# The first expert's seven chunks stand twice, in an If for up to 64 tokens and in an Else for more

## The chip, the cores and the metric

The kernel runs on one core of a Trainium2 chip. The metric is the device time of one execution, in microseconds (us). TensorE is written PE (its weight loads PEld, its sequencer PEq), VectorE DVE, ScalarE ACT, GpSimd POOL, and SP is the engine that issues the weight transfers. A profile is one execution under the hardware profiler.

## The reference, cut to what matters

The model is a two-layer decoder trunk over 256 tokens of width 1024. The change touches its last sublayer alone, a mixture of eight experts of which each token takes two:

```python
D_MODEL = 1024; SEQ = 256; N_EXPERTS = 8; TOP_K = 2; D_FF_EXPERT = 3584

def _swiglu(x, w1, w3, w2):
    return (jax.nn.silu(x @ w1) * (x @ w3)) @ w2

def _moe(x, w_router, w1, w3, w2):
    logits = (x @ w_router).astype(jnp.float32)
    top_v, top_i = lax.top_k(logits, TOP_K)
    gates = jax.nn.softmax(top_v, axis=-1)
    gate_full = jnp.sum(jax.nn.one_hot(top_i, N_EXPERTS, dtype=jnp.float32) * gates[..., None], axis=-2)
    out = jnp.zeros_like(x)
    for e in range(N_EXPERTS):
        y = _swiglu(x, w1[e], w3[e], w2[e])
        out = out + gate_full[..., e, None].astype(x.dtype) * y
    return out
...
        x = _layer_norm(DEEPNORM_ALPHA * x + f, ln_g[i, 1], ln_b[i, 1])
```

All weights are float32. The expert weights alone are 336 pieces of 1 MiB (128 x 2048 floats). With the reference's inputs the router sends 45, 78, 50, 86, 62, 60, 65 and 66 tokens to experts 0 to 7.

## The kernel before, in words

Everything ahead of the experts (state-space layer, dense feed-forward, attention) is left as it is. The stage in question is `experts` and the router code just ahead of it.

**Slots.** The tokens of an expert are gathered into a fixed number of slots, so that the matmuls have a fixed shape. Expert 0 is always taken first, with 96 slots. Experts 1 to 7 are sorted by their token counts while the kernel runs and put in places 1 to 7, whose slots are 64, 96, 64, 96, 96, 96, 64 (`CAPS`). If a place overflows, further passes at the end (an If on `cint[8]`) do the rest; that doesn't happen here.

**Chunks.** Each expert is cut in seven chunks (`NJ`) of 512 hidden columns, 56 in all, numbered `n`. A chunk takes six pieces: two of w1 and two of w3 (`up(n, 0, b)`, `up(n, 1, b)`), two of w2 (`down(n, b)`). With `b = 0` the first 64 slots are computed. An expert with 96 slots also has `b = 1` for the last 32 (`rest` for the up part). ACT takes the silu, DVE the product (`gated`), PE turns the result with transposes (`flip`, tile `ht`), and ACT copies it to `h`. The chunks overlap: `up` of chunk n stands ahead of `down` of chunk n-1.

**Pieces.** `Stream` holds a ring of 17 buffers `raw` (the tile `xx` is one of them, once). `take` hands out the next piece in order, `back` returns a buffer after its last matmul, and `load` issues the next transfer into it (line 74, on SP's queue, in the order of the program). The pieces of expert 0 have fixed addresses. Those of the other places depend on the sorting: `order` computes their starts into `cint`, and SP reads seven registers from there (line 1228) before it issues anything more.

**Around it.** After the router, `gather(0)` brings expert 0's tokens in with 32 matmuls (tile `gx`, line 1336). Small steps are kept in the list `side`, and `aside` runs one or two in each chunk: `gates`, `counts` (a matmul `cn` against ones and the first half of the sorting), `order`, `back` (for the scatter), the eight steps of `gather(1)` for places 1 to 4 and of `gather(2)` for places 5 to 7, and four `scatter` steps per finished expert. In chunk 5, POOL and ACT make the residual `x1` (lines 1472, 1473).

Of the kernel before, what the change touches and what calls it, by code (L numbers as in the profile page):

```python
# [45 lines left out]
class Stream:  # L46
# [31 lines left out]
    def add(self, raw=(), pairs=()):  # L78
        self.free.extend(raw)
        self.pairs.extend(pairs)  # L80
        self.load()

# [54 lines left out]
def trunk(ctx: ExitStack, tc: tile.TileContext, a, out, dbg=None):  # L137
# [45 lines left out]
    for n in range(E * NJ + 1):  # L183
        for m, qs in ((n, range(4)), (n - 1, (4, 5))):
            if 0 <= m < E * NJ:
                moe_seq += [(piece(m // NJ, 6 * (m % NJ) + q), 2048, False) for q in qs]
# [791 lines left out]
    with ExitStack() as e:  # L978
# [200 lines left out]
        cint = mo.tile([1, 9], I32, name="cint")  # L1179
# [22 lines left out]
        def counts(pp):  # L1202

            o = pp.tile([128, 8], F32, tag="tt", name="cn")
            for t in range(2):
                T.matmul(o, lhsT=ones, rhs=mask[:, t, :], start=(t == 0), stop=(t == 1))
            V.tensor_copy(out=by_e[:, 6, :], in_=o)
# [102 lines left out]
    def experts(ws, pas, pyy):  # L1310
        if pas:
            V.tensor_tensor(out=by_i[:, 2:4, :], in0=by_i[:, 2:4, :], in1=cst[:, None, 24:32].to_broadcast([128, 2, 8]), op=S_)
        with ExitStack() as e:
            pa = e.enter_context(pool(f"ps_a{pas}", bufs=1, space=PSUM))
            pto = None if pas else e.enter_context(pool("ps_to", bufs=1, space=PSUM))
            ptt = e.enter_context(pool(f"ps_tt{pas}", bufs=2, space=PSUM))
# [41 lines left out]

            def up(n, i, b):
# [8 lines left out]
                for hf in range(2):  # L1368
                    w = got[n, i][hf].rearrange("p (k c) -> p k c", c=512)
                    for k in range(4):  # L1370
                        kk = 4 * hf + k
                        tiles(ob[n, i], oc, x_[:, kk, x0 + lo:x0 + lo + m], w[:, k, :], m, 4 * m, not b and kk == 0, kk == 7)
                    if b or CAPS[n // NJ] == 64:
                        ws.back(got[n, i][hf])
                        ws.load()

            def flip(n):
                h_, q = hTs[n % 2], 3 if CAPS[n // NJ] > 64 else 2
# [5 lines left out]
            def down(n, b):  # L1384
                ee, j = divmod(n, NJ)
                h_ = hTs[n % 2]
                if b == 0:
                    got[n, 2] = [ws.take() for _ in range(2)]
                    if j == 0:
                        yp[ee] = [pyy.tile([128, 512 // (i + 1)], F32, tag=f"y{i}", name=f"y{i}") for i in range(2)]  # L1390
                for hf in range(2):
# [5 lines left out]
                    if b or CAPS[ee] == 64:  # L1397
                        ws.back(got[n, 2][hf])
                        ws.load()
# [17 lines left out]
            if pas:  # L1417
# [5 lines left out]
            def gated(n, i):  # L1423

                c, sl = 384 if CAPS[n // NJ] > 64 else 256, sls[n % 2]
# [5 lines left out]
            for n in range(NS + 1):  # L1431
                ee, j = divmod(n, NJ)
                big, bigp = (0 <= m < NS and CAPS[m // NJ] > 64 for m in (n, n - 1))

                def rest():
                    for i in range(2):
                        up(n, i, 1)
                        gated(n, i)

                if n < NS:  # L1440
                    up(n, 0, 0)
                    if not big:
                        gated(n, 0)
                if 0 < n < NS:
                    flip(n - 1)
                for _ in range(3 if n == 0 else 2):
                    aside()
                if n < NS:
                    up(n, 1, 0)
                    if not big:  # L1450
                        gated(n, 1)
                if n == NS - 1:
                    if big:
                        rest()
                    if not spare:
                        nc.sync.dma_start(out=ws.free[0], in_=gain_bias(3))
                        spare.extend(ws.free.pop(0).rearrange("p (a b) -> p a b", a=2) for _ in range(2))
                if n > 0:
                    down(n - 1, 0)
                    if n == NS - 1:  # L1460
                        flip(n)
                    if bigp:
                        down(n - 1, 1)
                    if (n - 1) % NJ == NJ - 1:
                        pe = (n - 1) // NJ
                        if pe < E - 1 or pas:
                            side.extend(out_steps(pe, yp.pop(pe)))
                if big and n < NS - 1:
                    rest()
                if n == 5 and not pas:  # L1470
                    for t in range(2):
# [5 lines left out]
                if j == 1 and ee + 1 < E:  # L1477
                    side.append(lambda q=ee + 1: back(q))
            while side:
                aside()  # L1480
            return yp.get(E - 1)
# [174 lines left out]
```

## Time and profile before

| | us |
|---|---|
| median of 3 runs (1542.08 to 1545.64) | 1544.24 |
| the profiled execution's own time | 1542.1 |
| its span, first to last instruction | 1540.2 |
| expert 0's first matmul starts | 674.5 |
| expert 0's first 17 pieces are issued by | 663.3 |
| the 18th piece is issued | 687.1 |
| PE busy over the span | 1465.0 |

The profile page has the span cut in 40 slices, with what the DMA engines moved in each. The trace behind it can be asked for the busy time of any stretch, for the instructions in order of time with what ended the idle time before each, and for one source line.

### The profile page before, as it was taken

What the parts mean: (1) busy time and instruction counts of PE and PEld (TensorE: products, weight loads), DVE (VectorE), ACT (ScalarE), POOL (GpSimd) and SP (SyncE); (2) the same over time, 40 slices, a digit from 0 to 9 for tenths busy, and PEclk for the clock granted to TensorE, in tenths of its full rate; (3) what the DMA queues carried; (4) which work ended last, traced back from release to release, by engine and by line L of the source; (5) the groups of instructions that cost most, each with busy time, mean ns of one, the idle gap of its engine ahead of it and who ended that gap; (6) DMA issues with size and microseconds to landing.
All of it is one profiled execution on the core that took longest, in us unless ns stands there. A gap on an engine that the chain in (4) does not pass through costs nothing. (4 is left out here: it accounts for less than half of the span.)

```text
span 1540.2 us, 34541 instructions
## 1 busy us (share of the span) xinstructions
PE 1465.0 (95%) x15235; PEld 1069.0 (69%) x15235; DVE 546.0 (35%) x1019; ACT 385.5 (25%) x633; POOL 117.5 (8%) x156
## 2 busy tenths in 40 slices
PE   7769899997999999999999999999899999999995
PEld 6657799996999999866665566654566666566552
DVE  9998844447566555541011010010100100100103
ACT  6525434333555545420010000010000100100100
POOL 0010573005000000000100000000000000000001
PEclk9989999999999999999999999999999999999998
DMA  6018389653535544458899999999999999989995
GB/s 254 7 35 298 143 279 255 205 183 139 181 135 181 178 151 173 162 237 365 329 375 426 426 426 424 425 426 426 426 424 426 424 390 400 390 350 389 397 426 220
DMA packets 68417, 458.41 MB, mean 298 GB/s; under 512 B 9041, under 2 KB 9716, under 8 KB 15780
## 3 DMA queue, kind: packets, MB, share of 16 engines
q1 hardware_dynamic: 62752, 443.63, 72.2%
q0 software_dynamic: 4272, 9.92, 2.3%
q10 hardware_dynamic: 1236, 2.58, 0.5%
q8 instruction: 122, 2.00, 0.5%
q14 instruction: 35, 0.29, 0.1%
HBM read 454.97 MB, written 3.48 MB: 298 GB/s over the span
## 5 line engine op out<-in xcount | busy, mean ns | idle before, releaser
L1356 PE MATMUL a<-raw,xe 128*32 128x128 f32 (+1 forms) x8016 | 537.7, 322 | 5.3 <-DMA raw<-in_moe 3.5
L1356 PEld LDWEIGHTS a<-raw,xe 128*32 128x32 f32 (+1 forms) x8016 | 371.9, 122 | 157.4 <-issue 28.6
L1356 PE MATMUL y<-raw,h 128*32 128x256 f32 (+1 forms) x2016 | 267.8, 476 | 2.9 <-DMA raw<-in_moe 2.4
L1429 DVE TENSOR_TENSOR sl<-sl,a 128x384 f32<-128x384 f32 (+1 forms) x56 | 28.3, 505 | 580.1 <-PE a L1356 579.8
L96 DVE TENSOR_TENSOR sp<-raw,sp 128x2048 fp32r<-128x2048 f32 (+1 forms) x83 | 181.7, 2195 | 98.1 <-ACT sp L95 98.1
L1356 PEld LDWEIGHTS y<-raw,h 128*32 128x32 f32 (+1 forms) x2016 | 96.8, 122 | 154.8 <-issue 123.6
L95 ACT CAST sp<-raw 128x2048 fp32r<-128x2048 f32 (+1 forms) x85 | 154.3, 1823 | 69.8 <-PE ab L911 32.8
L1085 PE MATMUL qkp<-xT,sp 128*128 128x256 f32 x1152 | 153.1, 287 | 0.0
L1427 ACT ACTIVATE sl<-a 128x384 f32<-128x384 f32 (+1 forms) x56 | 25.3, 451 | 507.4 <-PE a L1356 507.3
L1085 PEld LDWEIGHTS qkp<-xT,sp 128*128 128x128 f32 x1152 | 141.9, 191 | 1.9
L911 PE MATMUL ab<-xT,sp 128*128 128x256 f32 x960 | 117.2, 283 | 0.0
L911 PEld LDWEIGHTS ab<-xT,sp 128*128 128x128 f32 x960 | 116.6, 192 | 0.8
L955 PE MATMUL pv<-sp,xT 128*128 128x384 f32 x384 | 73.6, 345 | 3.7 <-ACT xT L782 2.0
L1382 ACT COPY h<-ht 128x384 f32<-128x384 f32 (+1 forms) x56 | 24.6, 439 | 200.8 <-PE ht L1381 200.1
L955 PEld LDWEIGHTS pv<-sp,xT 128*128 128x128 f32 x384 | 67.5, 193 | 6.6 <-DVE xT L783 3.5
L742 POOL TENSOR_TENSOR lr__1387<-lr__1387,mhalf 128x1 f32<-128x1 f32 x8 | 4.6, 569 | 849.4 <-DVE lr__1387 L741 849.4
L899 PE MATMUL facc<-sp,hh 128*128 128x512 f32 x176 | 54.4, 390 | 0.0
L675 PE MATMUL glu<-sp,xT 128*128 128x512 f32 x144 | 36.0, 408 | 4.4 <-DVE sp L96 4.4
L1406 DVE SCALAR_TENSOR_TENSOR xx<-so,by_i,xx 128x512 f32<-128x512 f32 x28 | 19.7, 746 | 55.0 <-PE so L1405 55.0
L457 PE MATMUL pu<-x0T,raw 128*128 128x256 f32 x128 | 29.7, 394 | 8.3 <-DMA raw<-in_w_in 8.3
L899 PEld LDWEIGHTS facc<-sp,hh 128*128 128x128 f32 x176 | 32.4, 188 | 6.3
L675 PEld LDWEIGHTS glu<-sp,xT 128*128 128x128 f32 x144 | 28.0, 196 | 11.9 <-DVE sp L96 5.3
(269 smaller groups left out, 1174.1 us busy)
## 6 DMA issues: line engine op xcount, KB each, us to landing
raw<-in_moe SPq DMA_DIRECT2D x334, 1024.0 KB, 19.0
raw<-in_ffn SPq DMA_DIRECT2D x33, 1024.0 KB, 6.8
raw<-in_qk SPq DMA_DIRECT2D x24, 1024.0 KB, 4.8
raw<-in_wv SPq DMA_DIRECT2D x16, 768.0 KB, 4.1
raw<-in_w_glu SPq DMA_DIRECT2D x8, 1024.0 KB, 5.2
raw<-in_w_o SPq DMA_DIRECT2D x4, 1024.0 KB, 4.8
raw<-in_w_in SPq DMA_DIRECT2D x3, 1024.0 KB, 10.4
skew<-vecs POOLq DMA_DIRECT2D x64, 36.0 KB, 4.5
```

The source lines that it names most:

```text
L95: self.nc.scalar.copy(out=h_, in_=t_)
L96: (eng or self.nc.vector).tensor_tensor(out=l_, in0=t_, in1=h_, op=ALU.subtract)
L457: T.matmul(pu[:, mm].rearrange("p a b -> p (a b)"), lhsT=w[:, k, mm * 128:mm * 128 + 128], rhs=x0T[:, k, :], start=(k == 0 and mm == mms[0 ...
L675: T.matmul(o[t], lhsT=s_, rhs=m_, start=(kk == 0 and i == 0), stop=(kk == 7 and i == 2))
L899: T.matmul(acc[t][n], lhsT=s_, rhs=m_, start=(j == 0 and f == 0 and ip == 0), stop=(j == NFP - 1 and f == 1 and ip == 2))
L911: T.matmul(o[:, f, :], lhsT=s_, rhs=m_, start=(k == 0 and ip == 0), stop=(k == 7 and ip == 2))
L955: T.matmul(ov[t], lhsT=s_, rhs=m_, start=(kk == 0 and ip == 0), stop=(kk == 7 and ip == 2))
L1085: T.matmul(o[:, qk, :], lhsT=s_, rhs=m_, start=(k == 0 and ip == 0), stop=(k == 7 and ip == 2))
L1356: T.matmul(o[n * g:n * g + n, oc:oc + c], lhsT=lhsT, rhs=rhs[:, c * g:c * g + c], start=start, stop=stop, tile_position=(0, n * g), skip_g ...
L1382: A.copy(out=h_[:, 0:q], in_=p_[:, 0:q])
L1427: A.activation(out=sl[:, 0:c], in_=ob[n, 0][:, 0:c], func=ACTF.Silu)
L1429: V.tensor_tensor(out=sl[:, 0:c], in0=sl[:, 0:c], in1=ob[n, 1][:, 0:c], op=M_)
```

## The change

The seven chunks of expert 0 are written twice. The router's counts move ahead of the last transposes of the router stage, so that the count of expert 0 stands in `cint[9]` early. `gates`, the sorting (`places`, `order`) and the one-hots of places 1 to 4 are then written right behind `gather(0)`, ahead of the chunks. Every engine reads `cint[9]` into a register and branches. In the If (count below 65), the chunks are computed with 64 slots, the second result tile is set to zero, and the buffers are returned in the same order as in the Else, which computes 96 slots as before. Behind both, the pipeline starts anew: `x1`, then all of `gather(1)` in one block, then the scatter of expert 0 among the chunks of place 1. The last two w2 pieces of expert 0 are loaded ahead of the first four of place 1.

```diff
-        for m, qs in ((n, range(4)), (n - 1, (4, 5))):
+        for m, qs in ((n, range(4)), (n - 1, (4, 5)))[::-1 if n == NJ else 1]:
...
+        cn = sml[:, 288:296]
+        for t in range(2):
+            T.matmul(cn, lhsT=ones, rhs=mask[:, t, :], start=(t == 0), stop=(t == 1), skip_group_check=True)
         rows(1, 1, ptn, "tr")
...
         V.tensor_copy(out=rank, in_=rk)
+        V.tensor_copy(out=by_e[:, 6, :], in_=cn)
+        V.tensor_copy(out=cint[:, 9:10], in_=cn[0:1, 0:1])
         one_hots(0, by_e)
...
+            def chunks(n0, n1, few=False):
+
+                for n in range(n0, n1 + 1):
+                    ee, j = divmod(n, NJ)
+                    cap, capp = (CAPS[m // NJ] if 0 <= m < NS and not few else 64 for m in (n, n - 1))
+                    big, bigp = cap > 64, capp > 64
+
+                    def rest():
+                        for i in range(2):
+                            if big:
+                                up(n, i, 1)
+                                gated(n, i, 384)
+                            else:
+                                for hf in range(2):
+                                    give(n, i, hf)
...
-            side.extend([lambda: back(0)] if pas else [gates, lambda: counts(ptt), order, lambda: back(0)])
...
-                if n == 5 and not pas:
-                    for t in range(2):
-                        Q.tensor_tensor(out=x1[t], in0=xh[0][:, t, :], in1=xh[1][:, t, :], op=A_)
-                        A.mul(out=x1[t], in_=x1[t], mul=ALPHA)
-                if j == 1 and ee in (0, 2):
-                    g_ = gather(1 + ee // 2)
-                    side.extend([lambda q=1 + ee // 2, f=g_[0]: (one_hots(q), f()), *g_[1:]])
...
+                gates()
+                places()
+                order()
+                one_hots(1)
+
+                n0 = nc.values_load(cint[0:1, 9:10], min_val=0, max_val=256)
+                pools.close()
+                state = ws.state()
+                with tc.If(n0 < 65) as cmp:
+                    renew()
+                    V.memset(yp[0][1], 0.0)
+                    chunks(0, NJ, True)
+                    pools.close()
+                end = ws.state()
+                ws.set(state)
+                with cmp.Else():
+                    renew()
+                    chunks(0, NJ)
+                    pools.close()
+                assert ws.same(end)
+                renew()
+                for t in range(2):
+                    Q.tensor_tensor(out=x1[t], in0=xh[0][:, t, :], in1=xh[1][:, t, :], op=A_)
+                    A.mul(out=x1[t], in_=x1[t], mul=ALPHA)
...
+            for f in gather(1):
+                f()
+            side.extend([lambda: back(0), lambda: back(1), *out_steps(0, yp.pop(0))])
+            chunks(NJ, NS)
```

On DVE, between the last copy of `gather(0)` and the first product of the chunks, the order before is this (`xe` holds the gathered tokens, `ex`, `top` and `by_e` belong to the gates, `cn` is the counts' matmul, `cint` the starts of the places, `sl` a chunk's product):

```order
L1338 COPY xe_6385<-gx 128x2x96 x2
L1195 TENSOR_SCALAR ex_6252<-ex_6251 128x2
...
L1200 TENSOR_TENSOR by_e<-top_6249,top_6250 128x16
L1207 COPY by_e<-cn 128x8
L1208 COPY by_e<-cst 128x8
...
L1223 CAST cint<-by_i 1x8
...
L1227 CAST cint<-key_6244 1x1
L1429 TENSOR_TENSOR sl_6375<-sl_6375,a_6548 128x384
```

and now this:

```order
L1306 COPY by_e<-sml 128x8
L1307 CAST cint<-sml 1x1
L1205 TENSOR_SCALAR O<-uni,by_e 128x96 x2
...
L1363 COPY xe_6389<-gx 128x2x96 x2
L1210 TENSOR_SCALAR ex_6252<-ex_6251 128x2
...
L1215 TENSOR_TENSOR by_e<-top_6249,top_6250 128x16
L1220 COPY by_e<-cst 128x8
...
L1235 CAST cint<-by_i 1x8
```

The copy of the counts has moved ahead of the gathering, two instructions there are new, and between the gates and the starts of the places no instruction reads a matmul of the chunks any more.

On PE, the count's matmul stands before among the chunk's first matmuls (tile `a`, weights `raw`):

```order
L1336 MATMUL gx<-O,xT_76 128x96
L1356 MATMUL a_6438<-raw_1365,xe_6385 64x256 x8
L1356 MATMUL a_6438<-raw_70,xe_6385 64x256 x8
L1206 MATMUL cn<-by_e,uni 128x8 x2
L1356 MATMUL a_6548<-raw_1366,xe_6385 64x256 x8
L1356 MATMUL a_6548<-raw_68,xe_6385 64x256 x8
L1356 MATMUL a_6438<-raw_1365,xe_6385 32x128 x16
```

Now a register load and a branch stand in its place, and the If goes on with the next chunk where the matmuls of 32 slots stood:

```order
L1361 MATMUL gx<-O,xT_76 128x96
L1520 TENSOR_LOAD cint
L1523 COMPARE_AND_BRANCH
L1381 MATMUL a_6565<-raw_1365,xe_6389 64x256 x8
L1381 MATMUL a_6565<-raw_70,xe_6389 64x256 x8
L1381 MATMUL a_6583<-raw_1366,xe_6389 64x256 x8
L1381 MATMUL a_6583<-raw_68,xe_6389 64x256 x8
L1381 MATMUL a_6605<-raw_3465,xe_6389 64x256 x8
```

On SP, the seven register loads of the places (line 1228 before, 1240 now) are followed by an eighth and the branch before the next piece is issued:

```order
L1240 TENSOR_LOAD cint
L1240 ISA x2
L1520 TENSOR_LOAD cint
L1520 ISA x2
L1523 COMPARE_AND_BRANCH
L74 DMA raw_1365<-in_moe 128x2048
```

The pieces and their buffers up to the branch are the same ones in the same order.

## Rows read from the trace of the kernel before

**Rows 1.** The page's head, and what DMA moved in each fortieth of the span.
```profile
span 1540.2 us, 34541 instructions
...
GB/s 254 7 35 298 143 279 255 205 183 139 181 135 181 178 151 173 162 237 365 329 375 426 426 426 424 425 426 426 426 424 426 424 390 400 390 350 389 397 426 220
```

**Rows 2.** Stretches: length, busy us of each engine (instructions), granted clock, DMA share, GB/s.
```profile
680.00:690.00 10.00, 10.00 (x188) 7.47 (x190) 4.12 (x17) 0.49 (x1) 0.00 (x0) 1.00 0.19 52
690.00:800.00 110.00, 109.88 (x1539) 70.17 (x1537) 7.63 (x20) 10.81 (x22) 4.69 (x2) 1.00 0.87 352
800.00:1000.00 200.00, 198.52 (x2301) 118.32 (x2298) 21.19 (x42) 17.40 (x39) 0.00 (x0) 1.00 1.01 426
```

**Rows 3.** Engine, line waited for: us in total, times, longest.
```profile
PE a L1356 <- DMA raw<-in_moe: 3.5, 6, 1.4
...
PE y L1356 <- DMA raw<-in_moe: 2.4, 5, 0.6
```

**Rows 4.** PE in order of time (start, us, instruction, idle before): two places where pieces came late.
```profile
882.52 1.94 PE L1356 MATMUL y<-raw,h 128*64 128x512 f32 x8 [0.45 <-DMA raw<-in_moe]
...
1085.30 1.95 PE L1356 MATMUL a<-raw,xe 128*64 128x256 f32 x16 [1.43 <-DMA raw<-in_moe]
```

**Rows 5.** The stretch of that second place, columns as in Rows 2.
```profile
1069.00:1093.00 24.00, 18.52 (x126) 8.99 (x126) 0.42 (x1) 1.03 (x3) 0.00 (x0) 1.00 1.01 426
```

**Rows 6.** PE in order of time: first matmuls of expert 0, and flips a chunk apart.
```profile
674.47 4.94 PE L1356 MATMUL a<-raw,xe 128*64 128x256 f32 x32
679.34 0.61 PE L1206 MATMUL cn<-by_e,uni 128*128 128x8 f32 x4
...
779.18 0.55 PE L1381 MATMUL ht<-idn,sl 128*128 128x128 f32 x3
...
795.88 0.55 PE L1381 MATMUL ht<-idn,sl 128*128 128x128 f32 x3
...
843.73 0.44 PE L1381 MATMUL ht<-idn,sl 128*128 128x128 f32 x2
844.09 3.67 PE L1356 MATMUL a<-raw,xe 128*64 128x256 f32 x32
...
854.59 0.44 PE L1381 MATMUL ht<-idn,sl 128*128 128x128 f32 x2
```

**Rows 7.** DVE in order of time: last of the gates, first copy of the counts, starts of places.
```profile
675.65 0.18 DVE L1200 TENSOR_TENSOR by_e<-top,top 128x16 f32<-128x16 f32 x1
679.99 0.17 DVE L1207 COPY by_e<-cn 128x8 f32<-128x8 f32 x1 [4.16 <-PE cn L1206]
...
682.60 0.16 DVE L1223 CAST cint<-by_i 1x8 int32<-1x8 f32 x1
```

**Rows 8.** SP: its register loads (ns min/median/max, first and last start), and the next issues.
```profile
L1228 SPq TENSOR_LOAD <-cint x7: 262/268/465, 682.8 to 686.5; - x7
...
687.08 2.98 SPq L74 DMA_DIRECT2D raw<-in_moe  x4
```

**Rows 9.** Single microseconds behind those issues, columns as in Rows 2.
```profile
688.00:689.00 1.00, 1.00 (x12) 0.68 (x10) 0.36 (x2) 0.00 (x0) 0.00 (x0) 1.00 0.93 147
689.00:690.00 1.00, 1.00 (x14) 0.64 (x12) 0.00 (x0) 0.00 (x0) 0.00 (x0) 1.00 0.84 336
```

**Rows 10.** The register load and branch of the If at the kernel's end, by source line.
```profile
L1518 PEldq TENSOR_LOAD <-cint x1: 483/483/483, 1518.5 to 1518.5; - x1
...
L1519 DVEq COMPARE_BRANCH  x1: 72/72/72, 1514.2 to 1514.2; - x1
...
L1519 PEldq COMPARE_BRANCH  x1: 3659/3659/3659, 1519.1 to 1519.1; - x1
L1519 DVEq EVENT_SEMAPHORE  x1: 21/21/21, 1519.8 to 1519.8; - x1
```

**Rows 11.** PE in order of time: two gathering steps, and the matmuls behind that branch.
```profile
707.72 1.67 PE L1336 MATMUL gx<-O,xT 128*128 128x320 f32 x8
...
1522.92 3.67 PE L1532 MATMUL so<-yw,OTg 64*128 64x512 f32 x8 [1.52 <-PEq L1519]
```

More of the change, by code (lines that the diff above doesn't have):

```diff
@@ L81, in add, with state, set, same @@
         self.load()
+    def state(self):
+        return {k: v.copy() if isinstance(v, (list, dict)) else v for k, v in vars(self).items()}
+    def set(self, state):
+        for k, v in state.items():
+            setattr(self, k, v.copy() if isinstance(v, (list, dict)) else v)
+    def same(self, state):
+        def ids(s):
+            return ([id(p) for p in s["free"]], *(sorted((k, id(p)) for k, p in s[n].items()) for n in ("loaded", "ready")),
+                    s["nload"], s["cur"])
+        return ids(vars(self)) == ids(state)
     def split(self, upto, eng=None):
@@ L1178, in trunk @@
         cube = mo.tile([128, 8, 8, 8], F32, name="cube")
-        cint = mo.tile([1, 9], I32, name="cint")
+        cint = mo.tile([1, 10], I32, name="cint")
         Ob = mo.tile([128, 2, SLOTS], F32R, name="O")
@@ L1200, in gates, with places @@
             V.tensor_tensor(out=gate, in0=o1, in1=o2, op=A_)
-        def counts(pp):
-            o = pp.tile([128, 8], F32, tag="tt", name="cn")
-            for t in range(2):
-                T.matmul(o, lhsT=ones, rhs=mask[:, t, :], start=(t == 0), stop=(t == 1))
-            V.tensor_copy(out=by_e[:, 6, :], in_=o)
+        def places():
+            o = by_e[:, 6, :]
             V.tensor_copy(out=by_e[:, 7, :], in_=cst[:, 0:8])
@@ L1357, in tiles, with give @@
                              tile_position=(0, n * g), skip_group_check=True)
+            def give(n, i, hf):
+                ws.back(got[n, i][hf])
+                ws.load()
             def up(n, i, b):
@@ L1373, in up, with flip @@
                     if b or CAPS[n // NJ] == 64:
[L1374 to L1378, printed above, removed]
+                        give(n, i, hf)
+            def flip(n, q):
+                h_ = hTs[n % 2]
                 p_ = ptt.tile([128, 3, 128], F32, tag="tt", name="ht")
@@ L1388, in down @@
                     got[n, 2] = [ws.take() for _ in range(2)]
-                    if j == 0:
+                    if ee not in yp:
                         yp[ee] = [pyy.tile([128, 512 // (i + 1)], F32, tag=f"y{i}", name=f"y{i}") for i in range(2)]
@@ L1397, in down @@
                     if b or CAPS[ee] == 64:
-                        ws.back(got[n, 2][hf])
-                        ws.load()
+                        give(n, 2, hf)
             def scatter(ee, t, i, o):
@@ L1420, in experts @@
                 f()
-            side.extend([lambda: back(0)] if pas else [gates, lambda: counts(ptt), order, lambda: back(0)])
-            def gated(n, i):
-                c, sl = 384 if CAPS[n // NJ] > 64 else 256, sls[n % 2]
-                if i == 0:
-                    A.activation(out=sl[:, 0:c], in_=ob[n, 0][:, 0:c], func=ACTF.Silu)
-                else:
-                    V.tensor_tensor(out=sl[:, 0:c], in0=sl[:, 0:c], in1=ob[n, 1][:, 0:c], op=M_)
[L1431 to L1469, printed above, removed]
-                if n == 5 and not pas:
-                    for t in range(2):
-                        Q.tensor_tensor(out=x1[t], in0=xh[0][:, t, :], in1=xh[1][:, t, :], op=A_)
-                        A.mul(out=x1[t], in_=x1[t], mul=ALPHA)
-                if j == 1 and ee in (0, 2):
-                    g_ = gather(1 + ee // 2)
-                    side.extend([lambda q=1 + ee // 2, f=g_[0]: (one_hots(q), f()), *g_[1:]])
-                if j == 1 and ee + 1 < E:
-                    side.append(lambda q=ee + 1: back(q))
@@ new lines, in experts @@
+            yp[0] = [pyy.tile([128, 512 // (i + 1)], F32, tag=f"y{i}", name=f"y{i}") for i in range(2)]
+            if pas:
+                chunks(0, NJ)
+            else:
+                gates()
[14 more added lines that the diff above has]
+                    renew()
+                    chunks(0, NJ)
+                    pools.close()
+                assert ws.same(end)
+                renew()
+                for t in range(2):
+                    Q.tensor_tensor(out=x1[t], in0=xh[0][:, t, :], in1=xh[1][:, t, :], op=A_)
+                    A.mul(out=x1[t], in_=x1[t], mul=ALPHA)
```

56 lines of the change are left out of this document (54 added, 2 removed).

## The prediction

> **What bounds the kernel now.** I read the stretches first, then who waited for whom, then single instructions. The page's line of transferred GB/s [rows 1] is uneven up to half of the span and then flat at 426, 425 and 424 for thirteen slices. The stretches say the same more sharply: 52 GB/s from 680 to 690 us, 352 from 690 to 800, 426 from 800 to 1000 [rows 2]. The reader is to see that 426 is the most the transfers ever do, and that they do less just where expert 0 is computed.
>
> PE is busy for 109.88 of the 110 us from 690 to 800 [rows 2], so there PE sets the pace: it computes 96 slots per chunk, frees buffers slowly, and the ring stays full. Two flips a chunk apart lie 795.88 - 779.18 = 16.7 us apart with 96 slots, about 16.4 without the small transpose step in that chunk, and 854.59 - 843.73 = 10.86 us with 64 [rows 6]. Six pieces of 1.0486 MB take 6 x 1.0486 / 0.426 = 14.77 us. So a chunk of 96 slots is bound by PE, and one of 64 by the transfers. The places alternate (96, 64, 96, 64, 96, 96, 96, 64): PE falls behind, then catches up with the transfers. It meets them twice, near 882.5 at the end of place 1 and up to 1093 at the end of place 3 [rows 4], and its waits for pieces are 3.5 + 2.4 = 5.9 us over the whole span [rows 3]. From 1093 on PE sets the end alone.
>
> The consequence carries the forecast: what is saved on PE alone in expert 0 ends at the first meeting. What moves both meetings is when the transfers got to run. **The gain is the time that DMA stood still during expert 0, less the time that it will still stand still.**
>
> **The change, part by part.**
>
> *The still time before.* From 680 to 800 us DMA moved 52 x 10 + 352 x 110 = 39,240 GB/s x us, that is 39.24 MB, for which 426 GB/s need 92.1 us. Of 120 us, 27.9 were lost. From 800 on nothing is lost up to both meetings [rows 1, 2].
>
> *The still time after, at its start.* The ring is full and landed before 680, so DMA waits for SP's next issue. SP issues at 687.08, behind seven register loads that begin at 682.8 [rows 8] and wait for the places' starts, written at 682.60 + 0.16 = 682.76 [rows 7]. That chain has a hole: DVE ends the gates at 675.83 and begins the sorting at 679.99, having waited 4.16 us for the counts' matmul [rows 7], which stands behind the first 32 matmuls of the chunk [rows 6]. In the changed order the counts come earlier and the hole closes. The two added matmuls (0.61 us, rows 6) and two added copies (0.17 us each by rows 7) stand ahead of the gathering; between 0 and 0.95 us of them delay it, I take 0.55, since the transposes behind them pass part of it on. So the gates end near 676.4, the starts are written 682.76 - 679.99 = 2.77 us later, less the copy now gone (about 0.1), at 679.1. SP then needs 687.08 - 682.76 = 4.3 us as before, and an eighth load: (686.5 - 682.8) / 6 = 0.6 us [rows 8]. First issue: 684.0. The flow follows the issue as it does now: in 688 to 690 DMA moved 147 + 336 = 483 [rows 9], worth 1.13 us of 426, so it began in effect at 688.87, 1.8 us behind 687.08. From 680 that leaves 5.8 us lost. **Gain: 27.9 - 5.8 = 22.1 us.**
>
> *Whether buffers are free in time.* With 64 slots PE frees six buffers in 10.86 us and DMA fills them in 14.77, so only the start can starve. The first four pieces of chunk 0 keep DMA until 685.8 + 9.85 = 695.6; the fifth issue is due 1.8 us before, at 693.8. PE's first 32 matmuls took 4.94 us where later ones take 3.67 [rows 6]; PE frees the first w2 buffer 4.94 + 3 x 3.5 + 0.36 + 1.75 = 17.6 us behind its start. Its start was 674.47 [rows 6]; with the 0.55 and a register load, 0.48 at the kernel's end [rows 10], it is 675.6. So 693.2: in time by 0.6 us. Every microsecond by which PE starts later than 676.2 costs one.
>
> *The branch.* The trace has one branch, at the kernel's end, and there every engine jumps over all the code of the passes. PE's took 3.66 us, DVE's own record is 0.07 us but its next instruction comes 5.5 us behind it [rows 10]. PE's matmuls stood for 1.52 us there [rows 11], since its sequencer had run ahead. Here the code of the If lies right behind the branch, so nothing is jumped over. Bounds: 0.05 us and 3.7 us on PE, 0.05 and 5.5 on SP. I take the low end, being nearest to the case in which the next instruction simply follows; the high end is a rival. The Trainium skill's page "Runtime: NRT & Kernel Launch", section "Instruction fetch mechanics", says that a taken branch to code outside the part held in the engine's instruction store must first fetch it, and that control flow is therefore expensive. That speaks against this change; by it the jump from the If's end over the Else is slow on PE, but the If's entry isn't, and the sum stands.
>
> *PE's saving and what it pays.* Expert 0 becomes 7 x (16.4 - 10.86) = 39 us shorter on PE. It pays a load and a branch (0.5 to 4.2 us), a pipeline drained once, and the jump over the Else (1.5 to 3.7, rows 10 and 11). `gather(1)` is moved, not added: two steps took 1.67 us [rows 11], so eight take 6.7 in a block, with the copies of ACT, behind its two multiplications for `x1`, and of DVE in turn. Taken together 3 to 10 us, so PE comes to the first meeting 29 to 36 us earlier, DMA 22.1: PE has 7 to 14 us in hand and waits for pieces through most of place 1. That is the cover of all these costs; without it they would go to the end one for one. POOL's two additions wait for the same buffer `xx` as before and nobody waits for POOL soon.
>
> *The rest.* The memset, the one-hots of places 1 to 4 on DVE (ahead of its branch) and the other order of six pieces at the seam lie in the same cover. From the first meeting on everything is as before, 22.1 us earlier, up to the end.
>
> **Sum.** 1542.1 - 22.1 = 1520.0 us against the profiled execution. The median of the runs, 1544.24, lies 2.1 us above it, so the forecast for the median is 1522.
>
> **Rivals.**
>
> *The entry of the If is slow.* For it: the 3.66 and 5.5 us of rows 10. Against it: those were jumps. On PE it costs 3.6 - 0.6 = 3.0 us (1525), on SP up to 5.5 (1527.5); the two overlap, since both delay the same flow.
>
> *TensorE loses its clock while it waits, and the kernel is slower.* In place 1 PE will work 10.86 of every 14.77 us, with a short wait at each piece. At the lower level, 1.2 GHz, a chunk would take twice 10.86, 21.7 us, which is 6.9 more than its pieces. The gain of 22.1 and the 5.9 us of waits that can give way are used up after four such chunks; with seven the end comes 7 x 6.9 - 28 = 20 us later than now: 1565. Against it: from 1069 to 1093 PE was busy 18.52 of 24 us, with waits of 0.4 to 1.4 us at every piece, and the granted clock stayed 1.00, the level of 2.4 GHz [rows 4, 5]. Place 1 has 74% where that stretch has 77%, only for longer. The Trainium skill's page "TensorE: Matmul & The Clock Gate", section "HAM oscillation — how this bites in real kernels", tells of kernels in which PE waits for a transfer at each tile and is throttled again at each, worst where the tile computes for less time than it waits. By that rule this rival could happen, to 1565 us; rows 5, with a wait at each piece and the full clock, speak against it.
>
> *The If doesn't do what it says.* If expert 0 had more than 64 tokens, the Else would run, PE would bound expert 0 as now, and the median would stay at 1541 to 1546. The reference's inputs give it 45.
>
> *PE sets the end after all.* If PE's work alone counted, the whole 39 us less 3 to 10 would be seen: about 1511. For it: PE's busy column is full nearly everywhere. Against it: 426 GB/s through both meetings.
>
> **How the numbers follow.** Forecast 0.66; slow entry 0.23; clock 0.04; Else 0.04; PE alone 0.03. A measurement of this kernel tells 0.2%, 3 us, from no change. Forecast, slow entry and PE alone are faster: 0.92. Else is the same: 0.04. Clock is slower: 0.04. The forecast's own range is 1518 to 1526: the 0 to 0.95 us at the gathering, the margin of 0.6 us and the runs' spread of -2.2 to +1.4. With the slow entry and an issue somewhat earlier or later than reckoned it is 1516 to 1530.
>
> **What would show it.** The If's matmuls without 32-slot forms; SP's first issue near 684 instead of 687.1; 420 GB/s and more from 690 to 800; waits of PE for pieces of some 15 to 30 us in all, most of them before 870; the first meeting's piece near 860 instead of 882.5; the end's 430 us as they were. Wrong it would be if SP issued behind 690, if the flow broke off behind the fourth piece, if PE's granted clock fell in place 1, or if the waits for pieces stayed at 6 us.

## The result, and the profile after

The changed kernel takes 1522.06 us (median; 1521.36 to 1522.38), the kernel before 1544.94 in the same comparison (1542.08 to 1546.07). The ratio is 0.9854, with a 95% interval of 0.9837 to 0.9871: **22.9 us less**. The profiled executions took 1521.36 and 1542.1 us, with spans of 1519.6 and 1540.2.

The page's head and line of transferred GB/s, and four stretches (columns as in [rows 2]), answer to [rows 1, 2]:

```profile
span 1519.6 us, 32295 instructions
...
GB/s 257 7 30 304 117 289 268 195 179 139 194 152 156 155 180 179 188 205 371 426 426 426 425 425 425 425 426 426 425 425 425 418 397 403 371 366 389 409 426 214
```
```profile
670.00:680.00 10.00, 10.00 (x48) 8.52 (x48) 4.29 (x17) 2.51 (x4) 0.00 (x0) 0.50 0.59 249
680.00:690.00 10.00, 10.00 (x86) 6.20 (x82) 3.93 (x17) 0.48 (x2) 0.00 (x0) 0.92 0.30 108
690.00:800.00 110.00, 105.82 (x762) 58.29 (x762) 12.77 (x27) 13.31 (x30) 4.68 (x2) 0.98 1.01 421
800.00:1000.00 200.00, 190.87 (x2229) 113.60 (x2227) 18.88 (x37) 17.05 (x38) 0.00 (x0) 1.00 1.01 425
```

The flat part at 425 or 426 GB/s now begins two slices earlier, and PE is no longer busy throughout. From 680 to 800 us DMA moved 108 x 10 + 421 x 110 = 47,390 GB/s x us, so 120 - 47,390 / 426 = 8.8 us were lost where 27.9 were before. That is a gain of 19.1. The waits for pieces, and the last one at each of the two meetings, answer to [rows 3, 4]:

```profile
PE a L1381 <- DMA raw<-in_moe: 8.3, 20, 0.7
PE y L1381 <- DMA raw<-in_moe: 5.4, 11, 0.6
```
```profile
863.90 1.94 PE L1381 MATMUL y<-raw,h 128*64 128x512 f32 x8 [0.40 <-DMA raw<-in_moe]
...
1073.36 1.94 PE L1381 MATMUL y<-raw,h 128*64 128x512 f32 x8 [0.41 <-DMA raw<-in_moe]
```

The last matmuls that wait for a piece at the second meeting stood here before:

```profile
1092.56 1.94 PE L1356 MATMUL y<-raw,h 128*64 128x512 f32 x8 [0.40 <-DMA raw<-in_moe]
```

PE ends its waits of place 1 at 863.9 (882.5 before, 18.6 us earlier) and those of place 3 at 1073.4 (1092.6 before, the same matmuls): 19.2 us earlier. The spans differ by 20.6; the 1.4 us between fall behind that point, where both kernels run the same work.

Why 8.8 us are still lost is seen at the router's end. PE and DVE in order of time, then SP's register loads and issues ([rows 6 to 8] of before):

```profile
668.13 1.00 PE L1301 MATMUL sml<-by_e,uni 128*128 128x8 f32 x4
668.99 1.09 PE L1257 MATMUL xb<-idn,x3T 128*128 128x128 f32 x4
669.85 7.17 PE L1361 MATMUL gx<-O,xT 128*128 128x96 f32 x32
676.96 12.90 PE L1381 MATMUL a<-raw,xe 128*64 128x256 f32 x96
```
```profile
677.06 0.36 DVE L1363 COPY xe<-gx 128x192 f32<-128x192 f32 x1 [3.06 <-PE gx L1361]
...
678.14 0.17 DVE L1215 TENSOR_TENSOR by_e<-top,top 128x16 f32<-128x16 f32 x1
...
680.76 0.16 DVE L1235 CAST cint<-by_i 1x8 int32<-1x8 f32 x1
```
```profile
L1240 SPq TENSOR_LOAD <-cint x7: 262/267/470, 681.0 to 684.6; - x7
...
685.91 14.04 SPq L74 DMA_DIRECT2D raw<-in_moe  x10
```

The hole in the sorting is closed: it starts as soon as the gates are there. But the gates end at 678.31, not 676.4, and SP issues at 685.91, not 684.0. And this is what PE did at the branch:

```profile
L1523 PEldq COMPARE_BRANCH  x2: 86/2922/5759, 673.6 to 752.5; - x2
```
```profile
752.45 3.65 PE L1381 MATMUL y<-raw,h 128*64 128x512 f32 x16 [0.52 <-ACT h L1410]
758.33 5.75 PE L1361 MATMUL gx<-O,xT 128*128 128x320 f32 x32 [2.23 <-issue]
```

The entry took PE's sequencer 86 ns. The jump from the If's end over the Else took it 5.76 us. PE still had matmuls to do during part of it and stood idle for 2.23.

### The profile page after: what moved, and what is told of

Read it like the earlier page. It is cut to its first block, busy times and chain, and to the rows that moved or that the text cites. A ratio compares the mean times of both kernels' runs of the same rounds, so it can differ in the third digit from the quotient of the medians.

```text
span 1519.6 us, 32295 instructions
## 1 busy us (share of the span) xinstructions
PE 1435.5 (94%) x14108; PEld 1043.3 (69%) x14108; DVE 545.2 (36%) x1021; ACT 384.4 (25%) x633; POOL 117.3 (8%) x156
## 5 line engine op out<-in xcount | busy, mean ns | idle before, releaser
L1381 PE MATMUL a<-raw,xe 128*64 128x256 f32 (+1 forms) x7152 | 516.3, 328 | 9.0 <-DMA raw<-in_moe 8.3
L1381 PEld LDWEIGHTS a<-raw,xe 128*64 128x64 f32 (+1 forms) x7152 | 351.6, 124 | 163.4 <-issue 25.6
L1381 PE MATMUL y<-raw,h 128*32 128x256 f32 (+1 forms) x1792 | 255.7, 488 | 6.4 <-DMA raw<-in_moe 5.4
L1450 DVE TENSOR_TENSOR sl<-sl,a 128x256 f32<-128x256 f32 (+1 forms) x56 | 27.3, 488 | 564.8 <-PE a L1381 564.5
L1381 PEld LDWEIGHTS y<-raw,h 128*32 128x32 f32 (+1 forms) x1792 | 89.9, 123 | 150.8 <-issue 118.2
L1448 ACT ACTIVATE sl<-a 128x256 f32<-128x256 f32 (+1 forms) x56 | 24.5, 438 | 503.9 <-PE a L1381 503.8
L1410 ACT COPY h<-ht 128x256 f32<-128x256 f32 (+1 forms) x56 | 23.8, 426 | 180.9 <-PE ht L1409 180.1
L626 PE MATMUL y<-p,cpad 128*32 128x127 f32 (+1 forms) x512 | 22.4, 331 | 16.0 <-DVE p L613 12.3
```

The costliest lines, as they stand in the source:

```text
L1381: T.matmul(o[n * g:n * g + n, oc:oc + c], lhsT=lhsT, rhs=rhs[:, c * g:c * g + c], start=start, stop=stop, tile_position=(0, n * g), skip_g ...
L1410: A.copy(out=h_[:, 0:q], in_=p_[:, 0:q])
L1448: A.activation(out=sl[:, 0:c], in_=ob[n, 0][:, 0:c], func=ACTF.Silu)
L1450: V.tensor_tensor(out=sl[:, 0:c], in0=sl[:, 0:c], in1=ob[n, 1][:, 0:c], op=M_)
```

## The experiments

The column "lost" is 120 x (1 - x / 426), from the GB/s x of the one stretch from 680 to 800 us in the trace of each kernel's one profiled execution (for the change that gives 8.7, where the two stretches above gave 8.8). The kernel before was timed beside each group of them, with medians of 1544.4 to 1545.6 us, and the ratios go by these.

| kernel | median us | ratio (95% interval) | GB/s 680 to 800 | lost us | median less lost |
|---|---|---|---|---|---|
| before | 1544.94 | 1 | 327 | 27.9 | 1517.0 |
| early_order, 96 slots | 1546.05 | 1.0009 (0.9999 to 1.0018) | 317 | 30.7 | 1515.4 |
| else_taken, 96 slots | 1541.16 | 0.9975 (0.9964 to 0.9985) | 336 | 25.4 | 1515.8 |
| **the change** | 1522.06 | 0.9854 (0.9837 to 0.9871) | 395 | 8.7 | 1513.4 |
| no_branch | 1521.32 | 0.9850 (0.9834 to 0.9867) | 395 | 8.7 | 1512.6 |
| gather3 | 1520.85 | 0.9846 (0.9833 to 0.9860) | 395 | 8.7 | 1512.2 |
| counts_late | 1523.48 | 0.9857 (0.9842 to 0.9872) | 385 | 11.5 | 1512.0 |
| sp_late | 1529.94 | 0.9903 (0.9888 to 0.9918) | 367 | 16.6 | 1513.3 |
| nb_late | 1520.62 | 0.9835 (0.9822 to 0.9848) | 397 | 8.2 | 1512.4 |
| nat | 1519.84 | 0.9830 (0.9816 to 0.9843) | 402 | 6.8 | 1513.0 |
| slots64 | 1518.51 | 0.9829 (0.9812 to 0.9845) | 402 | 6.8 | 1511.7 |
| late_regs64 | 1514.23 | 0.9798 (0.9785 to 0.9811) | 418 | 2.3 | 1511.9 |

The last column is the finding: over nine kernels with 64 slots, whose times spread by 15.7 us, it stays between 1511.7 and 1513.4. The time follows the microseconds in which the transfers stand still there.

**Is it the slots, or what was moved?** Two kernels keep 96 slots. The first is the change with another bound:

```diff
-                with tc.If(n0 < 65) as cmp:
+                with tc.If(n0 < 33) as cmp:
```


> The changed kernel with the bound of its condition at 33 in place of 65, so that the first expert's 45 tokens go through the Else: 96 slots, everything else as changed, the early counts, gates and sorting and the branch among it. Theory of the prediction (the gain is the transfers' lost time, and it is lost because a 96-slot chunk takes PE 16.4 us where its six pieces need 14.8): the transfers again wait for PE, the stretch 690 to 800 us moves some 350 GB/s and not 421, and the time is that of the kernel before less at most 4 us for what starts earlier, 1541 to 1546 us. Rival (the earlier sorting and the new order give the gain, and the slots only shorten PE's waits): as the changed kernel, 1522 us.

The second is the kernel before with the moves alone:

```diff
+        cn = sml[:, 288:296]
+        for t in range(2):
+            T.matmul(cn, lhsT=ones, rhs=mask[:, t, :], start=(t == 0), stop=(t == 1), skip_group_check=True)
...
+        V.tensor_copy(out=by_e[:, 6, :], in_=cn)
...
-            side.extend([lambda: back(0)] if pas else [gates, lambda: counts(ptt), order, lambda: back(0)])
+            if not pas:
+                gates()
+                counts()
+                order()
+            side.extend([lambda: back(0)])
```


> The kernel before with the moves alone: the two count matmuls behind the rank matmuls, gates, counts and the sorting of the experts ahead of the first chunk in place of among the side steps; 96 slots, no branch. Theory: SP issues some 1.2 us earlier and the first pieces land that much earlier, but with 96 slots PE sets the pace of the eight chunks, and PE starts its first chunk some 2.5 us later (the counts stand ahead of the gathering while the clock is at half): the stretch 690 to 800 us still moves 350 GB/s, and the time is within -3 and +3 us of the kernel before, 1542 to 1548. Rival (the early issue is the gain): 1522.

Measured: 1541.16 and 1546.05 us, both as the theory had it. The stretches of else_taken, then of early_order:

```profile
690.00:800.00 110.00, 110.00 (x1610) 68.59 (x1601) 4.37 (x8) 9.55 (x18) 4.69 (x2) 1.00 0.90 367
```
```profile
690.00:800.00 110.00, 109.88 (x1541) 70.08 (x1539) 8.18 (x21) 10.54 (x21) 4.69 (x2) 1.00 0.84 343
```

PE is again busy to the last tenth, and DMA at 367 and 343 GB/s. Without the 64 slots the moves bring nothing (early_order is 1.3 us slower by the medians), and the restructured kernel brings 3.6 us by its Else. In neither profiled execution did SP issue earlier than before (687.54 and 689.74 us against 687.08), so they don't show what an earlier issue would be worth with 96 slots.

The other side is 64 slots and nothing else:

```diff
-CAPS = tuple(96 if i == 0 or r < 4 else 64 for i, r in enumerate(RANKS))
+CAPS = tuple(96 if r < 4 else 64 for i, r in enumerate(RANKS))
```


> The kernel before with 64 slots for the first expert, fixed at compile time: no branch, no early counts, no early sorting, the pieces freed in the kernel's own order for 64 slots. Expert 0 has 45 tokens, so the same result is computed; of more than 64 the rest would go to the second pass. Theory (the transfers' still time): SP issues first at 687 us as before, 1.2 us later than in the changed kernel; four pieces then follow, and the fifth is freed in time since nothing delays the gathering; the first 110 us behind run at some 421 GB/s, and the gain is 17 to 20 us against the kernel before, 1525 to 1528 us, slower than the changed kernel by 0 to 4. Rival A (PE's work sets the time): 7 x (16.4 - 10.9) = 39 us less, 1506. Rival B (the branch and the restructuring cost microseconds on the path): faster than the changed kernel by more than 3 us, below 1519.

Measured: 1518.51, 26.3 us less than before and 3.6 less than the change. Rival A falls by 12 us. The theory's 17 to 20 us were too few, since it had SP issue first at 687. The time lies just past the point set for rival B, but the branch isn't the cause, as the next kernel shows. In slots64 the first two pieces are freed and issued, at 679.8 and 682.5 us, *ahead* of SP's register loads, since in the program's order they come first. SP then stands at the registers until 690.1:

```profile
679.79 3.03 SPq L74 DMA_DIRECT2D raw<-in_moe  x2
```
```profile
L1228 SPq TENSOR_LOAD <-cint x7: 262/268/465, 685.8 to 689.5; - x7
```

**What the branch costs.**

```diff
-                n0 = nc.values_load(cint[0:1, 9:10], min_val=0, max_val=256)
...
-                with tc.If(n0 < 65) as cmp:
-                    renew()
-                    V.memset(yp[0][1], 0.0)
-                    chunks(0, NJ, True)
-                    pools.close()
...
+                renew()
+                V.memset(yp[0][1], 0.0)
+                chunks(0, NJ, True)
+                pools.close()
```


> The changed kernel without its If and Else: the 64-slot chunks stand there unconditionally, the count is not read into registers, everything else is as changed. Theory: the entry took PE 86 ns, and the 5.8 us of the jump over the Else lie at 752 us, while PE waits for pieces for some 12 us between there and 864 us, so nothing of it reaches the end: 1522 us, within 1 us of the changed kernel. SP may issue up to 1 us earlier, since it reads one register less, and the end may come that much earlier. Rival (a jump on PE is paid in full): 1516 us.

Measured: 1521.32, 0.7 us below the change, with overlapping ranges (1520.32 to 1522.32). The branch's 5.8 us on PE are hidden.

**How much PE has in hand.** The second gathering three times in place of once, with the same result. Twice its 5.75 us are 11.5 us more of PE:

```diff
-            for f in gather(1):
+            for f in gather(1) + gather(1) + gather(1):
```


> The changed kernel with the second gathering's 32 matmuls run three times in place of once, right behind the If and Else: 2 x 5.75 = 11.5 us more of PE and some more of the DVE copies; the result is the same. Theory (PE has 8.5 us in hand from there to where it stops waiting for pieces at 864 us, by the sum of its waits for pieces and ends of buffers in the bins behind 770 us): the first 8.5 us vanish, the last 3 us delay the transfers from 860 us on, and what PE still has in hand up to 1073 us may take some of them: 1522 to 1526. Rival A (PE's work here is paid in full): +11.5, 1533.5. Rival B (PE has all the time it needs up to 1073 us): no change.

Measured: 1520.85, nothing lost. My 3 us fell; rival B holds. The waits of PE from 740 to 1100 us:

```profile
PE a L1381 <- DMA raw<-in_moe: 2.4, 6, 0.6
PE y L1381 <- DMA raw<-in_moe: 2.0, 4, 0.6
```

They sink from 13.7 to 4.4 us, and in place 1 PE no longer waits for a piece at all. The block took 18.28 us, 12.5 more than once, as the clock was low for part of it. The end of place 1 in gather3:

```profile
859.45 3.67 PE L1381 MATMUL a<-raw,xe 128*64 128x256 f32 x32
862.96 3.60 PE L1381 MATMUL y<-raw,h 128*64 128x512 f32 x16
```

The same matmuls end at 866.56 here and at 865.84 in the change, so 0.7 us are left of the 12.5. In the change 19 waits between 770 and 866 us add up to 8.5. The rest I had not counted: a wait costs more than the time that is listed for it. A group of 16 matmuls that waited for its piece takes 1.95 us up to its listed end, where two groups in a row have the next work start 862.96 - 859.45 = 3.51 us behind them, 1.75 each. By this estimate 19 waits cost 19 x 0.2 = 3.8 us more, and 8.5 + 3.8 is what vanished.

The transfers did not feel that the buffers came late (426 GB/s from 820 to 865 us). The time from issue to landing of the pieces issued from 780 to 820 us, in the changed kernel and then in gather3, shows why:

```profile
DMA to landing us min/median/max: 19.5/19.7/20.3
```
```profile
DMA to landing us min/median/max: 12.6/17.2/19.4
```

In the change SP issued 17 pieces in these 40 us, one in about 2.5, so a piece that takes 19.5 us to land stands behind some seven others, by estimate. When PE frees buffers late, that queue gets shorter first, and DMA runs on.

**Does the end follow SP's first issue?** Sixteen more register loads on SP, whose values are not used:

```diff
+            for _ in range(16):
+                nc.values_load(cint[0:1, 1:2], engines=[mybir.EngineType.SP], min_val=0, max_val=(E - 1) * PIECES)
```


> The changed kernel with 16 more register loads on SP ahead of its first issue of the first expert's pieces, at 0.5 to 0.6 us each 8 to 10 us. They change no result. Theory (the end follows the transfers, and these follow SP's first issue): the first issue comes at 694 to 696 us; behind it the transfers no longer wait for the fifth buffer, which the changed kernel lost some 2.4 us to; so the end is later by 5.5 to 8 us, 1527.5 to 1530. Rival (PE sets the end, the transfers have time in hand): within 1 us of the changed kernel. Second rival (the transfers' delay is paid in full, no starvation in the changed kernel): +8 to +10.

Measured: 1529.94, 7.9 us later, with the first issue at 694.84, 8.9 later. The theory holds; about 1 us was absorbed by the still time behind the fourth piece.

**The delay ahead of the gathering.** The counts behind the router's last transposes:

```diff
+        rows(1, 1, ptn, "tr")
         cn = sml[:, 288:296]
         for t in range(2):
             T.matmul(cn, lhsT=ones, rhs=mask[:, t, :], start=(t == 0), stop=(t == 1), skip_group_check=True)
-        rows(1, 1, ptn, "tr")
...
         parts(1, 1)
+        V.tensor_copy(out=by_e[:, 6, :], in_=cn)
+        V.tensor_copy(out=cint[:, 9:10], in_=cn[0:1, 0:1])
```


> The changed kernel with the two count matmuls moved from ahead of the last router transposes to behind them, and their two copies behind the one-hot parts of the first gathering: 0.94 us of DVE's wait for PE at 669 us and what follows from it. Theory (the step that the prediction sized too small, 2.5 us in place of 0.55, is the counts at half clock ahead of the gathering): the gathering copies end near 674.6 us as in the kernel before, in place of 677.1, SP issues first at 683.5 to 684.5 in place of 685.9, the first chunk starts 1.5 to 2.5 us earlier, and the end comes 1.5 to 3.5 us earlier than in the changed kernel: 1518.5 to 1520.5. Rival (the clock that stands at half there, and not the place of the counts, delays the gathering): within 0.5 us of the changed kernel.

Measured: 1523.48, no gain; the expectation fell. The trace says why the edit could not tell the two apart:

```profile
672.25 7.03 PE L1361 MATMUL gx<-O,xT 128*128 128x96 f32 x32 [1.69 <-DVE cint L1309]
```

The counts share the tile `sml` with the rest of the router, and the gathering's PSUM tile comes free only when DVE's last copy out of it is done. By putting the copies later I made PE wait 1.69 us for them, and SP issued first at 688.16. What the counts cost is read from slots64 instead, which has none there (its 32 gathering matmuls are 64 columns wide, but took 7.13 us against 7.17 in the change):

```profile
676.18 0.29 DVE L1338 COPY xe<-gx 128x128 f32<-128x128 f32 x1 [3.12 <-PE gx L1336]
```

The router stood at the same place in both (the last search for a maximum at 666.59 and 666.62 us), and so did the clock. The changed kernel's copy is at 677.06: 0.88 us for the counts.

**What the last 8.7 us are.** Two pieces of them were left: SP's wait for the sorting, and the fifth piece. Two kernels take them up, both without the If and Else, so that they are read against no_branch. In nat the first expert's pieces are given back as each product has read them, in place of in the order of 96 slots:

```diff
-                    if b or CAPS[n // NJ] == 64:
+                    if b or CAPS[n // NJ] == 64 or n < NJ and not pas:
...
-                    if b or CAPS[ee] == 64:
+                    if b or CAPS[ee] == 64 or ee == 0 and not pas:
...
-                        elif few:
-                            for hf in range(2):
-                                give(n - 1, 2, hf)
```


> The changed kernel without its If and Else (64-slot chunks unconditionally), with the first expert's pieces given back as each product has read them, in place of at the end of a chunk as 96 slots need it. The register loads on SP stay where they are, so SP issues first at 686 us. Theory (order of freeing): the fifth buffer is then free by 692 us, the transfers do not stand still behind the fourth piece, and the end comes 1.5 to 2.5 us earlier than in the kernel without the branch: 1519 to 1520. Rival (the time behind the fourth piece is hidden): within 0.5 us of 1521.3.

In nb_late the freeing stays, and SP's register loads move:

```diff
+        def registers():
+
             first.extend([0] + [nc.values_load(cint[0:1, i:i + 1], engines=[mybir.EngineType.SP], min_val=0,
                                                max_val=(E - 1) * PIECES) for i in range(1, E)])
             ws.load()
...
+                    if n == 2 and not pas:
+                        registers()
```


> The changed kernel without its If and Else (64-slot chunks unconditionally), and with SP's seven register loads moved behind the third chunk: four pieces can then be issued as PE frees them, from 680.5 us on. But the freeing stays in the order that the change gave the 64-slot chunks, which is that of 96 slots: the fifth and sixth buffers that SP waits for are those of the first chunk's second product, freed at 695.6 and 697.3 us. Theory (order of freeing): the transfers start 5 us earlier, and stand still longer ahead of the fifth, which is issued at the same 695.6 to 696: the end within 1 us of the kernel without the branch, 1520.5 to 1522.5. Rival (SP's first issue sets the end): 1516 to 1517.

Measured: nat 1519.84, nb_late 1520.62, both as expected. Eight microseconds of the change, of nat and of nb_late, in this order:

```profile
692.00:700.00 8.00, 8.00 (x62) 4.20 (x60) 0.42 (x1) 0.00 (x0) 0.00 (x0) 1.00 1.00 400
```
```profile
692.00:700.00 8.00, 8.00 (x62) 4.20 (x60) 0.42 (x1) 0.00 (x0) 0.00 (x0) 1.00 1.01 427
```
```profile
692.00:700.00 8.00, 8.00 (x62) 4.17 (x58) 0.42 (x1) 0.00 (x0) 0.00 (x0) 1.00 0.52 202
```

In nat the flow doesn't break off. In nb_late SP issues first at 680.8, 5 us sooner, and the sooner start is given back while everyone waits for the fifth buffer, issued at 695.7 us as ever. Either edit alone is worth 1.5 us at most (no_branch has 1521.32); the runs of nat lie clear of no_branch's, those of nb_late overlap with them.

Both together, without the early counts, is slots64 with SP's register loads behind the third chunk, where the first sorted piece has yet to be asked for:

```diff
+                if n == 2 and not pas:
+                    registers()
```


> The kernel before with 64 slots for the first expert at compile time, and with SP's seven register loads for the sorted experts moved from behind the sorting to behind the third chunk (they are needed from piece 42 on). In the kernel with 64 slots alone SP issued two pieces at 679.8 and 682.5 us, as PE freed them, stood at the registers until 690.1, and the transfers were still from 687 to 691.7 us. Theory (what is left of the gain is the stretch in which SP waits for the sorting, not PE): SP issues on as PE frees pieces, the transfers run through from 681.6 us, and the end comes 3.5 to 5.5 us earlier than with 64 slots alone: 1513 to 1515. Rival (PE's own work and its later start at half clock are by then as late as the transfers): within 1.5 us of 1518.5.

Measured: 1514.23, 7.8 us less than the change and 31.3 less than before: **the fastest here**. SP issues from 679.6 on as PE frees, and the stretch from 680 to 800 stands at 418 GB/s (395 in the change):

```profile
680.00:800.00 120.00, 120.00 (x906) 67.83 (x902) 17.71 (x49) 13.86 (x32) 4.69 (x2) 1.00 1.01 418
```
```profile
680.00:800.00 120.00, 115.82 (x846) 64.49 (x844) 16.69 (x44) 13.79 (x31) 4.68 (x2) 0.98 0.95 395
```

With more than 64 tokens for expert 0 it would take the kernel's further pass, which the change avoids.

## Why the prediction was right, and where it was not

The forecast was 1522.0 us and the median is 1522.06, closer than its parts. The transfers gave 19.2 us, not 22.1. Behind the second meeting came 1.4 us that no term had. And the profiled execution of before lay 2.8 us below its median in the new comparison, that of after 0.7 below its own: 19.2 + 1.4 + 2.8 - 0.7 = 22.7, against 22.9 measured. The errors cancelled, and that the sum came out to 0.1 us is luck.

**The pace and the two meetings** are right. The gain is what the transfers lost, it shows at both meetings (18.6 and 19.2 us), and PE's 39 us saved show nowhere. The table shows it over 14 us of lost time at a slope near one.

**The gathering's delay** is the mis-sized term: 0.55 us (bounds 0 to 0.95) where it was 677.06 - 674.57 = 2.5, outside its bounds. It has three parts. The router itself stood 0.61 us later in the profiled execution (last maximum at 666.62 instead of 666.01), ahead of anything changed. The counts took 0.88 against 0.55, as they ran at half clock (their four matmuls 1.00 us; in no_branch, where the clock was still full, 0.59). The remaining 1.0 is the clock: a low stretch lies there in every kernel, and here it began earlier, at 668 us, and lasted until nearly 682. The stretch from 676 to 678, before and after:

```profile
676.00:678.00 2.00, 2.00 (x18) 1.13 (x16) 0.00 (x0) 0.00 (x0) 0.00 (x0) 0.73 0.02 8
```
```profile
676.00:678.00 2.00, 2.00 (x11) 1.53 (x13) 0.87 (x6) 1.26 (x1) 0.00 (x0) 0.50 0.07 29
```

slots64 has the low clock at the same times without early counts, and no_branch, whose router stood 1.5 us later, has it begin 3 us later with them, so it isn't the counts that move it. I took all durations there at the clock of one execution.

**SP's first issue**, 685.91 for 684.0, is later by just this; its own steps were right (the sorting 2.6 us for 2.7, the loads 5.0 for 4.9). **The flow behind it** followed as reckoned. **The fifth issue** failed: PE started at 676.96 where 676.2 was the limit, and at half clock until nearly 682, so the fifth piece was issued at 695.6 for 693.8. By nat's stretch that cost 8 x (427 - 400) / 426 = 0.5 us up to 700, and by 688 to 712 us, 406 GB/s against 426, 1.1 us in all. "Wrong it would be if the flow broke off behind the fourth piece": it did, at a small price. So 1.9 us of late issue and 1.1 behind the fourth piece are the 3.0 us by which the transfers' gain fell short.

**The branch.** The low end was right: 86 ns at the entry. else_taken shows the same branch taken the other way, over the If's code:

```profile
L1523 PEldq COMPARE_BRANCH  x1: 4780/4780/4780, 674.8 to 674.8; - x1
```

There PE's first matmul of the chunks came 1.64 us behind the gathering, where in the change it followed at once. The branch ended at 679.58 and that matmul began at 679.80; the profile names a DVE instruction that ended at 679.59, so how much of the 1.64 is the branch's isn't settled. That the jump at the If's end is hidden was right too (no_branch). PE's idle time of 2.23 us there lies within the 1.5 to 3.7 that were named; the sequencer's 5.76 us lie above its 3.66 in rows 10. The Trainium skill's page "Runtime: NRT & Kernel Launch", section "Instruction fetch mechanics", says that a taken branch to code outside the part that the engine holds must wait until that code is fetched. This trace agrees on PE: 86 ns into the code that follows, 4.78 and 5.76 us over a passage. That the time goes into fetching no run shows.

**PE's time in hand** was named as 7 to 14 us, and waits as 15 to 30. The waits were 13.7, below that. But each wait that gives way saves some 0.2 us of matmul time besides (gather3), so the cover was thicker than the waits, and the queue ahead of DMA kept the transfers going meanwhile.

**The clock** stayed at 1.00 from 800 to 1000 us, where PE waits for many pieces; the rival for 1565 us did not come. PE worked some 1.95 us on a piece there and waited 0.2 to 0.7, so what that rival calls the worst, more waiting than work, did not happen here. Between the router's end and there it fell once, at the seam:

```profile
768.00:770.00 2.00, 0.88 (x4) 0.47 (x4) 1.53 (x5) 0.49 (x2) 0.00 (x0) 1.00 1.02 418
770.00:772.00 2.00, 2.00 (x13) 1.18 (x14) 0.00 (x0) 0.37 (x1) 0.00 (x0) 0.61 1.00 422
772.00:774.00 2.00, 2.00 (x14) 1.17 (x12) 0.00 (x0) 0.00 (x0) 0.00 (x0) 0.54 1.03 434
774.00:776.00 2.00, 2.00 (x22) 1.35 (x20) 0.42 (x1) 0.00 (x0) 0.00 (x0) 1.00 1.02 430
```

PE had idled 2.23 us at the jump and 1.19 just before 768.9, and then ran some 3 us at half speed. Without the branch (no_branch) PE has the second pause and not the first, and the whole stretch from 756 to 800 is at 1.00. This too was hidden.

**Behind the second meeting** the prediction has 430 us, the same in both kernels. From the start of the last matmul that waits for a piece to the end of the span it was 447.6 before and 446.2 after. PE's waits from 1094 us to the end, before and then after:

```profile
PE so L1532 <- PEq L1519: 1.5, 1, 1.5
PE a L1356 <- issue: 1.3, 2, 0.9
```
```profile
PE so L1599 <- PEq L1586: 0.9, 1, 0.9
PE a L1381 <- issue: 0.6, 1, 0.6
```

The wait at the kernel's last branch is 0.6 us shorter, and waits without a named cause are 0.7 shorter: nearly all of the 1.4. Over the twelve profiled executions this stretch is 445.6 to 448.3 us long, so 1.4 is within what they differ by. Why these waits differ stays open.

The three kernels with 96 slots lie 2 to 5 us higher in the table's last column for reasons of this kind. Before, the profiled execution lay 2.8 us below the median, and the stretch behind the second meeting was 1.4 longer. In early_order that stretch took 448.3, as the eight matmuls behind the last branch took 6.37 us and not 3.67, with a granted clock of 0.50 at their end. else_taken lost 5 us from 800 to 1000 (415 GB/s), which the column doesn't count. Counted up to the start of the last matmul that waits for a piece, less what the transfers lost from 680 us to there, all twelve executions come to 1062 to 1065 us.

## What to carry to other kernels

Where an engine catches up with the transfers later on, count what the transfers lost, not what the engine saved; engine work added behind that point was free here at 12.5 us, against 13.7 of waits, while the queue ahead of DMA got shorter and did not run dry; where it stops being free was not measured. Look for what an issuing queue waits for that it doesn't need yet: here seven register loads for later experts held up pieces whose addresses were known, and moving them was worth 4 us more than slots64 alone, while early counts and early sorting brought nothing (early_order, and nat beside slots64), and the branch cost nothing that the runs can tell. When buffers are freed in the order of one shape and used in that of another, the transfers stall at the first buffer out of order, and an earlier start is given back there.

## What the runs showed of the hardware

- A compare-and-branch on PE took 86 ns into code that follows (the change), 4.78 us at the same place when it went over the If's seven chunks (else_taken), and 5.76 us over the Else's (the change). SP's and DVE's own records in the change are 41 to 60 ns, so a branch's record on one engine says nothing of another's.
- The low-clock stretch at the router's end lasted from about 670 to 677 us in the profile of before and from 668 to nearly 682 in those of the change and of slots64. Two executions whose router stands 0.6 us apart can differ by 1 us in the same 32 matmuls from this alone.
- In the change a piece landed 4.7 us behind its issue when nothing was ahead of it (the shortest from 675 to 700 us), and 19.5 us or more with a full queue (780 to 820).
- A group of 16 matmuls that waited for its piece took PE 1.95 us up to its listed end, and 1.75 in a row without waits (the change and gather3), so a listed wait of 0.4 us cost about 0.6, by estimate.
